# A grouped 3x3 convolution on one core: one weight tile for both pipelines, the first x rows in two pieces, the second pipeline 18 slots behind

## The chip, the cores and the metric

The kernel runs on one core of a Trainium2 chip. The metric is the device time of one execution in microseconds, and the number that counts is the median over several executions. A run's profile is that of one execution: it has a span (first to last instruction) that is a little shorter than that execution's own time.

## What is computed

`x` is 16 x 64 x 64 x 64 (image, channel, row, column), `weight` is 128 x 8 x 3 x 3, there are 8 groups, and everything is float32. Group g makes 16 output channels of 8 input channels, with a border of zeros:

```python
for g in range(groups):
    for b in range(batch):
        for co in range(16):
            for ci in range(8):
                for kh in range(3):
                    for kw in range(3):
                        output[b, g * 16 + co] += weight[g * 16 + co, ci, kh, kw] * \
                            x_pad[b, g * 8 + ci, kh:kh+h, kw:kw+w]
```

The input is 16.8 MB, the output 33.6 MB.

## The kernel before

**Tiles.** Two images have 128 channels together, so one tile holds one row of `x` (reshaped to 1024 x 4096) per partition. `xn[i]` are rows 128i to 128i+127, for i = 0 to 3: images 2i and 2i+1. `xs[i]` start at row 544 + 128i: images 8 and up, shifted by 32 partitions, so that one image's first half of channels lies in another quarter of the array than in `xn`. The missing 32 rows (512 to 543) sit in the last quarter of `xs[3]`. All are bf16 in SBUF. `ob` are eight output buffers, each of one whole image (128 channels x 4096 float32, 2 MB). The eight PSUM banks belong to two pipelines, four each.

**Loads (lines 103 to 154).** GpSimd issues 17 loads, each half of a tile (32 of 64 rows), that cast float32 to bf16 on the way; 128 partitions of them are 0.5 MB in bf16 and 1 MB read. They wait for nothing except two short waits for the masks. Two loads go another way: the first half of `xn[0]` is fetched by SP as float32 into the first half of output buffer `ob[7]` (`raw`, line 116) and is cast by ACT in two copies (line 121), and the weights are fetched on ACT's queue (line 118).

**Weight preparation (lines 158 to 187).** DVE multiplies the weights with a 0/1 mask of groups into `E`, five blocks of 32 columns for every tap (line 162). TensorE transposes 128 columns of `E` per tap, at two offsets, into PSUM (line 175): 9 transposes for `wN` and 9 for `wS`. DVE copies `wN` and ACT copies `wS` out of PSUM (line 185). The result is, per tap, a matrix of 32 input channels (four groups) by 64 output channels in each quarter.

**The main loop (lines 200 to 294).** Pipeline 0 makes images 0 to 7 from `xn` and `wN`, pipeline 1 images 8 to 15 from `xs` and `wS`. A *set* is 16 rows of an image pair: two steps j of 8 rows, two images, so four banks of 512 columns. Per tap and step, a pipeline has four matmuls of 32 x 64, one in each quarter of the array's rows; the two pipelines use the opposite halves of the columns, so eight such matmuls can be in the array at a time. The order is written out by hand in *slots*: one tap of one set, 9 slots for a set and 3 without matmuls (`PERIOD` = 12), 16 sets per pipeline. Pipeline 1 runs `LAG` = 6 slots behind, so that each evicts its banks while the other works.

After a set's last tap, `finish` (line 254) evicts four banks, ACT and DVE in turns (line 268). An eviction that begins an image pair waits for the store that last used its output buffer. After the last set of an image pair, SP issues the two stores (line 278), 16 KB per partition; for the first image pair of each pipeline (i = 0) each image is stored in two halves, 8 KB per partition. SP's queue holds the stores in program order and waits for each one's evictions. Images take the eight buffers in turn, pipeline 0's pair, then pipeline 1's.

All transfers run on the same 16 DMA engines.

Of the kernel before, what the change touches and what calls it, by code (L numbers as in the profile page):

```python
# [7 lines left out]
FP32 = mybir.dt.float32  # L8
BF16 = mybir.dt.bfloat16
ALU = mybir.AluOpType  # L10


@with_exitstack
def kernel(
    ctx: ExitStack,
    tc: tile.TileContext,
    x: bass.AP,
    weight: bass.AP,
    groups: int,
    out: bass.AP,  # L20
):
    nc = tc.nc

    B, C, H, W = x.shape
    CO, CIg, K, _ = weight.shape
    G = groups
    COg = CO // G
    HW = H * W
    T = K * K
    assert (B, C, CO, K, G, H, W) == (16, 64, 128, 3, 8, 64, 64)  # L30

    R = 8
    NCH = H // R
    HALF = HW // 2

    NOB = 8

    pool = ctx.enter_context(tc.tile_pool(name="sb", bufs=1))
    psum = ctx.enter_context(tc.tile_pool(name="psum", bufs=1, space=bass.MemoryType.PSUM))

    xn = [pool.tile([128, H, W], BF16, name=f"xn{i}") for i in range(4)]
    xs = [pool.tile([128, H, W], BF16, name=f"xs{i}") for i in range(4)]
    ob = [pool.tile([128, HW], FP32, name=f"ob{i}") for i in range(NOB)]
    w_sb = pool.tile([128, CIg * T], FP32, name="w_sb")
    mask = pool.tile([128, G], FP32, name="mask")
    ident = pool.tile([128, 128], BF16, name="ident")
    E = pool.tile([128, T, 160], BF16, name="E")
    wN = pool.tile([128, T, 128], BF16, name="wN")
    wS = pool.tile([128, T, 128], BF16, name="wS")
    banks = [psum.tile([128, 512], FP32, name=f"bank{i}") for i in range(8)]  # L50

    with tc.tile_critical():  # L52
        program(nc, x, weight, out, xn, xs, ob, w_sb, mask, ident, E, wN, wS, banks)


class Order:
# [23 lines left out]
        return self.sem, self.n  # L80


def program(nc, x, weight, out, xn, xs, ob, w_sb, mask, ident, E, wN, wS, banks):
    H = W = 64
    HW, HALF, T, G, CIg, COg, R = H * W, H * W // 2, 9, 8, 8, 16, 8
    NOB = len(ob)
# [7 lines left out]
    def sem(name):  # L94
        s = nc.alloc_semaphore(name)
        sems.append(s)
        return s
# [13 lines left out]
                landed[t.name, q, h] = (s, 16)  # L111


    raw = ob[NOB - 1][:, 0:HALF]
    s_raw = sem("raw")
    nc.sync.dma_start(raw, xr[0:128, 0:HALF]).then_inc(s_raw, 16)
    s_w = sem("w")
    nc.scalar.dma_start(w_sb, weight.rearrange("co ci kh kw -> co (ci kh kw)")).then_inc(s_w, 16)
    ACT.wait((s_raw, 16))
    for h in (0, 16):  # L120
        raw_read = ACT.done(nc.scalar.copy(  # L121
            xn[0][:, h : h + 16, :].rearrange("p h w -> p (h w)"), raw[:, h * W : (h + 16) * W],
        ))
        for q in range(4):
            for r in range(h, h + 16):
                landed[xn[0].name, q, r] = raw_read

    m1 = DVE.done(nc.vector.memset(mask, 1.0))  # L128
    m2 = DVE.done(nc.vector.memset(ident, 0.0))  # L129
    for h0, h1 in ((0, 32), (32, 64)):  # L130
        if h0 > 0:
            load(xn[0], 0, 0, 128, h0, h1)
        load(xs[0], 544, 0, 128, h0, h1)
        if h0 == 0:
            POOL.wait(m1)
            m3 = POOL.done(nc.gpsimd.affine_select(  # L136
                out=mask, in_=mask, compare_op=ALU.is_ge, fill=0.0,
                base=0, channel_multiplier=1, pattern=[[-COg, G]],
            ))
            POOL.wait(m2)  # L140
            m4 = POOL.done(nc.gpsimd.affine_select(  # L141
                out=ident, in_=ident, compare_op=ALU.not_equal, fill=1.0,
                base=0, channel_multiplier=1, pattern=[[-1, 128]],
            ))
            POOL.wait(m3)
            m5 = POOL.done(nc.gpsimd.affine_select(  # L146
                out=mask, in_=mask, compare_op=ALU.is_ge, fill=0.0,
                base=COg - 1, channel_multiplier=-1, pattern=[[COg, G]],
            ))
        load(xs[3], 512 - 96, 96, 128, h0, h1)  # L150
    for i in range(1, 4):
# [3 lines left out]

    wv = w_sb.rearrange("co (ci t) -> co t ci", t=T)
    DVE.wait((s_w, 16), m5)
    for r in range(5):  # L160
        g0 = 4 * (r % 2)
        e = DVE.done(nc.vector.tensor_mul(  # L162
            E[:, :, 32 * r : 32 * r + 32].rearrange("p t (g c) -> p t g c", c=CIg),
            wv.unsqueeze(2).to_broadcast([128, T, 4, CIg]),
            mask[:, g0 : g0 + 4].unsqueeze(1).unsqueeze(3).to_broadcast([128, T, 4, CIg]),
        ))
    PE.wait(e, m4)
    free = [None] * 8
    w_need = {}
    for k, (wt, off) in enumerate(((wN, 0), (wS, 32))):  # L170
        for g, t0 in enumerate(range(0, T, 4)):
            n = min(4, T - t0)
            b = 4 * k + g
            for t in range(n):
                ins = nc.tensor.matmul(  # L175
                    banks[b][:, 128 * t : 128 * t + 128],
                    E[:, t0 + t, off : off + 128],
                    ident,
                    start=True, stop=True,
                )  # L180
            p = PE.done(ins)
            dst = wt[:, t0 : t0 + n, :].rearrange("p t c -> p (t c)")
            eng, copy = ((DVE, nc.vector.tensor_copy), (ACT, nc.scalar.copy))[k]
            eng.wait(p)
            free[b] = eng.done(copy(dst, banks[b][:, 0 : 128 * n]))  # L185
            for t in range(n):
                w_need[wt.name, t0 + t] = free[b]

    outf = out.rearrange("b co h w -> b co (h w)")
    taps = [(1, 1)] + [(a, b) for a in range(3) for b in range(3) if (a, b) != (1, 1)]
    pe = nc.tensor
    stored = [nc.alloc_semaphore(f"st{i}") for i in range(NOB)]
    uses = [0] * NOB
# [3 lines left out]
    class Pipe:  # L200
# [5 lines left out]
        def streams(self, i):  # L206

            if self.k == 0:
                return [(q // 2, wN, xn[i], q, q % 2) for q in range(4)]
            return [  # L210
                (0, wS, xs[i], 0, 1), (1, wS, xs[i], 1, 0),
                (1, wS, xs[i], 2, 1), (0, wS, xs[i - 1], 3, 0),
            ]

        def matmuls(self, st, k, j):
# [6 lines left out]
            v0 = w0 - (kw - 1)  # L222
            nr, nw = hi - lo, w1 - w0
            left = {0: 2, 1: 2}
            for im, wt, xt, q, half in self.streams(i):
                b = self.banks[j][im]
                pos = dict(tile_position=(32 * q, 64 * half))
                w_ap = wt[32 * q : 32 * q + 32, 3 * kh + kw, 64 * half : 64 * half + 64]
                x_ap = xt[32 * q : 32 * q + 32, lo:hi, w0:w1]
                o_ap = banks[b].rearrange("p (h w) -> p h w", w=W)[  # L230
                    64 * half : 64 * half + 64, o0 : o0 + nr, v0 : v0 + nw
                ]
                if j == 0:
                    PE.wait(w_need[wt.name, 3 * kh + kw])
                    pe.ldweights(w_ap, **pos)  # L235
                PE.wait(
                    free[b] if k == 0 else None,
                    landed[xt.name, q, lo], landed[xt.name, q, hi - 1],
                )
                ins = pe.add_instruction(  # L240
                    mybir.InstMatmult(
                        name=nc.get_next_instruction_name(),
                        engine=mybir.EngineType.PE,
                        start_tensor_calc=k == 0, stop_tensor_calc=k == T - 1,
                        tile_size=(32, 64), ldweights=False, **pos,
                        ins=[pe.lower_ap(x_ap, opt=False), pe.lower_ap(w_ap, opt=False, for_matmul_weights=True)],
                        outs=[pe.lower_ap(o_ap)],
                    )
                )
                left[im] -= 1  # L250
                if k == T - 1 and left[im] == 0:
                    self.full[j, im] = PE.done(ins)

        def finish(self, st):
            i, s = st // 4, st % 4
            if s == 0:
                self.slots = [(nob[0] + im) % NOB for im in range(2)]
                self.empty = [(stored[slot], 16 * uses[slot]) if uses[slot] else raw_read for slot in self.slots]
                self.wrote = [[], []]
                nob[0] += 2  # L260
            for j in range(2):
# [7 lines left out]
                    self.wrote[im].append(free[b])  # L269
                nev[0] += 1  # L270
            nev[0] += 1
            if s == 1 and i == 0 or s == 3:
                o0, o1 = (0 if s == 1 or not (i == 0) else HALF), HALF * (s + 1) // 2
                for im in range(2):
                    slot = self.slots[im]
                    img = 2 * i + 8 * self.k + im
# [2 lines left out]
                    uses[slot] += 1  # L279

    pipes = (Pipe(0), Pipe(1))
    PERIOD, LAG, NSETS = T + 3, (T + 3) // 2, 16
    for slot in range(PERIOD * NSETS + LAG):
        live = []
        for p, lag in zip(pipes, (0, LAG)):
# [60 lines left out]
```

## Time and profile before

| What | Value |
|---|---|
| median of 9 runs | 128.67 us (128.47 to 129.14) |
| the profiled execution's own time | 128.77 us |
| its span | 127.0 us |
| TensorE busy | 86.9 us, 2322 matmuls |
| DVE, ACT, GpSimd busy | 46.1, 39.1, 9.8 us |
| HBM read and written | 16.81 MB, 33.55 MB |
| first matmul of the convolution | 11.59 us |
| first store issued | 22.52 us |
| last eviction begins | 100.28 us |

The chain that ended last, as the page gives it:

```profile
PE 45%; DMA 27%; DVE 5%; issue 1%; ACT 0%; SPq 0%; ACTq 0%; DVEq 0%
PE bank L240 43%; DMA out_dram<-ob 23%; DMA w_sb<-in_weight_dram 4%; DVE ob L268 3%; DVE E L162 2%; PE bank L175 2%; ACT ob L268 0%; ACTq L341 0%; DVEq L74 0%; SPq L278 0%; SPq L52 0%
```

The first line is by engine, the second by line of the code. The chain follows waits for semaphores; a transfer that lies behind other transfers in a queue is not resolved into them, so the time in which DMA was full has to be read from the other rows. In the rows of slices, each digit is the busy share of one fortieth of the span in tenths. GB/s counts the bytes that arrive: a casting load counts with its bf16 bytes, half of what it reads. The rows of stretches (windows) give, for each engine, busy time with its number of instructions in brackets, and then TensorE's granted clock, the mean busy share of the 16 DMA engines and GB/s. That share can pass 1 by a few per cent, since the packets of an engine overlap a little.

### The profile page before, as it was taken

The page shows a single profiled execution, that of the slowest core. Times are in us where ns is not written, and L with a number is a line of the kernel's source. Part 1 is how long each engine was busy: PE and PEld are TensorE (multiplying, and loading weights), DVE is VectorE, ACT ScalarE, POOL GpSimd, SP SyncE. Part 2 cuts the span into 40 slices and gives each one's busy share as a digit, 9 for nine tenths or more (in the row PEclk, how much of TensorE's full clock was granted, in tenths as well). Part 3 has the DMA queues.
Part 4 walks back from the last instruction along what each step waited for, and adds up shares of the span by engine and source line. Part 5 has one row for each costly group of instructions (what it writes and reads, how often), then busy time and mean ns, then how long its engine had stood idle before and what let it go on. Part 6 is the DMA issues. An engine that isn't in the chain of part 4 may idle for free.

```text
span 127.0 us, 3785 instructions
## 1 busy us (share of the span) xinstructions
PE 86.9 (68%) x2322; PEld 39.9 (31%) x1170; DVE 46.1 (36%) x74; ACT 39.1 (31%) x70; POOL 9.8 (8%) x24
## 2 busy tenths in 40 slices
PE   0009999999999989997939999999999600000000
PEld 0006425355453535452214445443354200000000
DVE  0094055445644464644224644555446500000000
ACT  4063045335433444433034633525336300000000
POOL 5995000000000000000000000000000000000000
PEclk9999999999999999999999999999999995555555
DMA  3999999999999999999999999999999999999950
GB/s 44 330 215 210 214 215 209 217 288 316 319 316 304 321 307 324 321 310 312 432 418 436 423 428 428 408 438 433 423 413 418 449 428 428 418 438 444 428 222 10
DMA packets 5375, 42.74 MB, mean 336 GB/s; under 512 B 752, under 2 KB 752, under 8 KB 2672
## 3 DMA queue, kind: packets, MB, share of 16 engines
q1 hardware_dynamic: 3024, 34.60, 65.2%
q0 software_dynamic: 2192, 7.87, 30.8%
q8 instruction: 13, 0.21, 0.6%
q10 hardware_dynamic: 144, 0.04, 0.4%
q14 instruction: 2, 0.02, 0.0%
HBM read 16.81 MB, written 33.55 MB: 396 GB/s over the span
## 4 chain that ended last, share of the span: by engine, by line
PE 45%; DMA 27%; DVE 5%; issue 1%; ACT 0%; SPq 0%; ACTq 0%; DVEq 0%
PE bank L240 43%; DMA out_dram<-ob 23%; DMA w_sb<-in_weight_dram 4%; DVE ob L268 3%; DVE E L162 2%; PE bank L175 2%; ACT ob L268 0%; ACTq L341 0%; DVEq L74 0%; SPq L278 0%; SPq L52 0%
## 5 line engine op out<-in xcount | busy, mean ns | idle before, releaser
L240 PE MATMUL bank<-xs,wS 32*64 32x504 bf16 (+3 forms) x1152 | 72.1, 373 | 3.1 <-ACT ob L268 2.1
L240 PE MATMUL bank<-xn,wN 32*64 32x504 bf16 (+3 forms) x1152 | 71.0, 376 | 0.9 <-DVE ob L268 0.9
L268 DVE COPY ob<-bank 128x512 f32<-128x512 f32 x64 | 41.5, 687 | 48.4 <-PE bank L240 42.0
L268 ACT COPY ob<-bank 128x512 f32<-128x512 f32 x64 | 34.6, 589 | 54.3 <-PE bank L240 45.9
L235 PEld LDWEIGHTS <-wS 32*64 32x64 bf16 x576 | 26.2, 104 | 23.2 <-issue 13.7
L235 PEld LDWEIGHTS <-wN 32*64 32x64 bf16 x576 | 19.2, 105 | 27.1 <-issue 22.7
L175 PE MATMUL bank<-ident,E 128*128 128x128 bf16 x18 | 2.1, 313 | 9.6 <-DVE E L162 9.6
L105 POOL DMA_DIRECT2D xs<-in_x_dram x10 | 5.7, 573 | 1.0 <-SPq L52 1.0
L162 DVE TENSOR_TENSOR E<-w_sb,mask 128x288 bf16<-128x288 f32 x5 | 2.9, 654 | 5.3 <-DMA w_sb<-in_weight_dram 5.3
L175 PEld LDWEIGHTS bank<-ident,E 128*128 128x128 bf16 x18 | 1.8, 146 | 9.6 <-DVE E L162 9.6
L105 POOL DMA_DIRECT2D xn<-in_x_dram x7 | 4.1, 581 | 0.0
L121 ACT CAST xn<-ob 128x1024 bf16<-128x1024 f32 x2 | 2.0, 1042 | 4.2 <-DMA ob<-in_x_dram 4.2
L185 ACT CAST wS<-bank 128x512 bf16<-128x512 f32 (+1 forms) x3 | 1.2, 487 | 2.3 <-PE bank L175 2.3
L185 DVE CAST wN<-bank 128x512 bf16<-128x512 f32 (+1 forms) x3 | 1.5, 550 | 0.7 <-PE bank L175 0.7
L121 ACT ACT_TABLE_LOAD x1 | 1.3, 1283 | 1.4 <-SPq L52 1.4
L128 DVE MEMSET mask<- 128x8 f32 x1 | 0.1, 65 | 1.1 <-SPq L52 1.1
L141 POOL TENSOR_SCALAR_AFFINE_SELECT ident<-ident 128x128 bf16<-128x128 bf16 x1 | 0.3, 305 | 0.0
L136 POOL TENSOR_SCALAR_AFFINE_SELECT mask<-mask 128x8 f32<-128x8 f32 x1 | 0.2, 211 | 0.1
L146 POOL TENSOR_SCALAR_AFFINE_SELECT mask<-mask 128x8 f32<-128x8 f32 x1 | 0.2, 197 | 0.0
L327 POOL MEMSET const-float32-0.0<- 128x1 f32 x1 | 0.1, 99 | 0.3 <-issue 0.3
L129 DVE MEMSET ident<- 128x64 uint32 x1 | 0.1, 112 | 0.0
L327 POOL MEMSET const-bfloat16-1.0<- 128x1 bf16 x1 | 0.1, 102 | 0.0
(2 smaller groups left out, 0.2 us busy)
## 6 DMA issues: line engine op xcount, KB each, us to landing
out_dram<-ob SPq DMA_DIRECT2D x12, 2048.0 KB, 20.2
out_dram<-ob SPq DMA_DIRECT2D x8, 1024.0 KB, 22.6
xn<-in_x_dram POOLq DMA_DIRECT2D x7, 512.0 KB, 23.0
xs<-in_x_dram POOLq DMA_DIRECT2D x6, 512.0 KB, 17.5
ob<-in_x_dram SPq DMA_DIRECT2D x1, 1024.0 KB, 5.9
xs<-in_x_dram POOLq DMA_DIRECT2D x2, 384.0 KB, 48.1
xs<-in_x_dram POOLq DMA_DIRECT2D x2, 128.0 KB, 9.3
w_sb<-in_weight_dram ACTq DMA_DIRECT2D x1, 36.0 KB, 5.6
```

The costliest lines, as they stand in the source:

```text
L105: nc.gpsimd.dma_start(t.rearrange("p h w -> p (h w)")[p0:p1, h0 * W : h1 * W], xr[row0 + p0 : row0 + p1, h0 * W : h1 * W],).then_inc(s, 16)
L121: raw_read = ACT.done(nc.scalar.copy(xn[0][:, h : h + 16, :].rearrange("p h w -> p (h w)"), raw[:, h * W : (h + 16) * W],))
L136: m3 = POOL.done(nc.gpsimd.affine_select(out=mask, in_=mask, compare_op=ALU.is_ge, fill=0.0, base=0, channel_multiplier=1, pattern=[[-COg, ...
L141: m4 = POOL.done(nc.gpsimd.affine_select(out=ident, in_=ident, compare_op=ALU.not_equal, fill=1.0, base=0, channel_multiplier=1, pattern=[ ...
L146: m5 = POOL.done(nc.gpsimd.affine_select(out=mask, in_=mask, compare_op=ALU.is_ge, fill=0.0, base=COg - 1, channel_multiplier=-1, pattern= ...
L162: e = DVE.done(nc.vector.tensor_mul(E[:, :, 32 * r : 32 * r + 32].rearrange("p t (g c) -> p t g c", c=CIg), wv.unsqueeze(2).to_broadcast([ ...
L175: ins = nc.tensor.matmul(banks[b][:, 128 * t : 128 * t + 128], E[:, t0 + t, off : off + 128], ident, start=True, stop=True,)
L185: free[b] = eng.done(copy(dst, banks[b][:, 0 : 128 * n]))
L235: pe.ldweights(w_ap, **pos)
L240: ins = pe.add_instruction(mybir.InstMatmult(name=nc.get_next_instruction_name(), engine=mybir.EngineType.PE, start_tensor_calc=k == 0, st ...
L268: free[b] = eng.done(copy(ob[slot][:, o0 : o0 + 512], banks[b]))
L327: nc = _bacc.Bacc("TRN2", target_bir_lowering=False, num_devices=1)
```

## The change

There are four edits.

- **One weight tile.** `wN` and `wS` become one tile `wt`, which both pipelines use. DVE no longer multiplies with a mask ahead of the transposes; it copies the weights, repeated 16 times, into `wb` (three copies for 4, 4 and 1 taps). TensorE transposes 9 times, and DVE multiplies with a mask of 128 x 4 as it takes the result out of PSUM (three products). The mask is made of a tile of 128 x 4 x 4 by the same two selects of GpSimd and a sum of DVE. The taps change their order to 4, 5, 6, 7, 0, 1, 2, 3, 8, and the weights are stored in that order.
- **The first x rows in two pieces.** SP fetches 8 rows and then 24 rows of `xn[0]`'s first half, after the weights' issue in the program; ACT casts them in four copies of 8 rows.
- **The first stores.** Only pipeline 0's first image pair is stored in halves; pipeline 1's first pair is stored whole like all others.
- **The lag.** `LAG` goes from 6 to 18 slots: a whole period more.

The diff, without the tiles' declarations and signatures:

```diff
@@ -111,31 +111,34 @@
                 landed[t.name, q, h] = (s, 16)
 
 
-    raw = ob[NOB - 1][:, 0:HALF]
-    s_raw = sem("raw")
-    nc.sync.dma_start(raw, xr[0:128, 0:HALF]).then_inc(s_raw, 16)
+    raw = ob[NOB - 1]
     s_w = sem("w")
     nc.scalar.dma_start(w_sb, weight.rearrange("co ci kh kw -> co (ci kh kw)")).then_inc(s_w, 16)
-    ACT.wait((s_raw, 16))
-    for h in (0, 16):
-        raw_read = ACT.done(nc.scalar.copy(
-            xn[0][:, h : h + 16, :].rearrange("p h w -> p (h w)"), raw[:, h * W : (h + 16) * W],
-        ))
-        for q in range(4):
-            for r in range(h, h + 16):
-                landed[xn[0].name, q, r] = raw_read
-
-    m1 = DVE.done(nc.vector.memset(mask, 1.0))
+    raw_read = []
+    for h0, h1 in ((0, 8), (8, 32)):
+        s_raw = sem(f"raw{h0}")
+        nc.sync.dma_start(raw[:, h0 * W : h1 * W], xr[0:128, h0 * W : h1 * W]).then_inc(s_raw, 16)
+        for h in range(h0, h1, 8):
+            ACT.wait((s_raw, 16))
+            raw_read = [ACT.done(nc.scalar.copy(
+                xn[0][:, h : h + 8, :].rearrange("p h w -> p (h w)"), raw[:, h * W : (h + 8) * W],
+            ))]
+            for q in range(4):
+                for r in range(h, h + 8):
+                    landed[xn[0].name, q, r] = raw_read[0]
+
+    m1 = DVE.done(nc.vector.memset(mask4, 1.0))
     m2 = DVE.done(nc.vector.memset(ident, 0.0))
     for h0, h1 in ((0, 32), (32, 64)):
         if h0 > 0:
             load(xn[0], 0, 0, 128, h0, h1)
         load(xs[0], 544, 0, 128, h0, h1)
         if h0 == 0:
+
             POOL.wait(m1)
             m3 = POOL.done(nc.gpsimd.affine_select(
-                out=mask, in_=mask, compare_op=ALU.is_ge, fill=0.0,
-                base=0, channel_multiplier=1, pattern=[[-COg, G]],
+                out=mask4, in_=mask4, compare_op=ALU.is_ge, fill=0.0,
+                base=0, channel_multiplier=1, pattern=[[-32, 4], [-CIg, 4]],
             ))
             POOL.wait(m2)
             m4 = POOL.done(nc.gpsimd.affine_select(
@@ -144,8 +147,8 @@
             ))
             POOL.wait(m3)
             m5 = POOL.done(nc.gpsimd.affine_select(
-                out=mask, in_=mask, compare_op=ALU.is_ge, fill=0.0,
-                base=COg - 1, channel_multiplier=-1, pattern=[[COg, G]],
+                out=mask4, in_=mask4, compare_op=ALU.is_ge, fill=0.0,
+                base=CIg - 1, channel_multiplier=-1, pattern=[[32, 4], [CIg, 4]],
             ))
         load(xs[3], 512 - 96, 96, 128, h0, h1)
     for i in range(1, 4):
@@ -155,42 +158,40 @@
 
 
 
+    taps = [(t // 3, t % 3) for t in (4, 5, 6, 7, 0, 1, 2, 3, 8)]
+    DVE.wait(m5)
+    r = DVE.done(nc.vector.tensor_reduce(
+        out=mask, in_=mask4.rearrange("p q g -> p g q"), op=ALU.add, axis=mybir.AxisListType.X,
+    ))
+    DVE.wait((s_w, 16))
     wv = w_sb.rearrange("co (ci t) -> co t ci", t=T)
-    DVE.wait((s_w, 16), m5)
-    for r in range(5):
-        g0 = 4 * (r % 2)
-        e = DVE.done(nc.vector.tensor_mul(
-            E[:, :, 32 * r : 32 * r + 32].rearrange("p t (g c) -> p t g c", c=CIg),
-            wv.unsqueeze(2).to_broadcast([128, T, 4, CIg]),
-            mask[:, g0 : g0 + 4].unsqueeze(1).unsqueeze(3).to_broadcast([128, T, 4, CIg]),
+    groups = ((0, 4, 4), (4, 0, 4), (8, 8, 1))
+    filled = [DVE.done(nc.vector.tensor_copy(
+        wb[:, k0 : k0 + n, :].rearrange("p t (g c) -> p t g c", c=CIg),
+        wv[:, t0 : t0 + n, :].unsqueeze(2).to_broadcast([128, n, 16, CIg]),
+    )) for k0, t0, n in groups]
+    PE.wait(m4)
+    free = [None] * 8
+    w_need = []
+    for b, (k0, t0, n) in enumerate(groups):
+        PE.wait(filled[b])
+        for k in range(n):
+            ins = nc.tensor.matmul(
+                banks[b][:, 128 * k : 128 * k + 128], wb[:, k0 + k, :], ident, start=True, stop=True,
+            )
+        p = PE.done(ins)
+        DVE.wait(p, r)
+        free[b] = DVE.done(nc.vector.tensor_mul(
+            wt[:, k0 : k0 + n, :].rearrange("p t (h g c) -> p (t h) g c", h=2, g=4),
+            banks[b][:, 0 : 128 * n].rearrange("p (t g c) -> p t g c", g=4, c=COg),
+            mask.unsqueeze(1).unsqueeze(3).to_broadcast([128, 2 * n, 4, COg]),
         ))
-    PE.wait(e, m4)
-    free = [None] * 8
-    w_need = {}
-    for k, (wt, off) in enumerate(((wN, 0), (wS, 32))):
-        for g, t0 in enumerate(range(0, T, 4)):
-            n = min(4, T - t0)
-            b = 4 * k + g
-            for t in range(n):
-                ins = nc.tensor.matmul(
-                    banks[b][:, 128 * t : 128 * t + 128],
-                    E[:, t0 + t, off : off + 128],
-                    ident,
-                    start=True, stop=True,
-                )
-            p = PE.done(ins)
-            dst = wt[:, t0 : t0 + n, :].rearrange("p t c -> p (t c)")
-            eng, copy = ((DVE, nc.vector.tensor_copy), (ACT, nc.scalar.copy))[k]
-            eng.wait(p)
-            free[b] = eng.done(copy(dst, banks[b][:, 0 : 128 * n]))
-            for t in range(n):
-                w_need[wt.name, t0 + t] = free[b]
+        w_need += [free[b]] * n
 
 
 
 
     outf = out.rearrange("b co h w -> b co (h w)")
-    taps = [(1, 1)] + [(a, b) for a in range(3) for b in range(3) if (a, b) != (1, 1)]
     pe = nc.tensor
     stored = [nc.alloc_semaphore(f"st{i}") for i in range(NOB)]
     uses = [0] * NOB
@@ -206,10 +207,10 @@
         def streams(self, i):
 
             if self.k == 0:
-                return [(q // 2, wN, xn[i], q, q % 2) for q in range(4)]
+                return [(q // 2, xn[i], q, q % 2) for q in range(4)]
             return [
-                (0, wS, xs[i], 0, 1), (1, wS, xs[i], 1, 0),
-                (1, wS, xs[i], 2, 1), (0, wS, xs[i - 1], 3, 0),
+                (0, xs[i], 0, 1), (1, xs[i], 1, 0),
+                (1, xs[i], 2, 1), (0, xs[i - 1], 3, 0),
             ]
 
         def matmuls(self, st, k, j):
@@ -222,16 +223,16 @@
             v0 = w0 - (kw - 1)
             nr, nw = hi - lo, w1 - w0
             left = {0: 2, 1: 2}
-            for im, wt, xt, q, half in self.streams(i):
+            for im, xt, q, half in self.streams(i):
                 b = self.banks[j][im]
                 pos = dict(tile_position=(32 * q, 64 * half))
-                w_ap = wt[32 * q : 32 * q + 32, 3 * kh + kw, 64 * half : 64 * half + 64]
+                w_ap = wt[32 * q : 32 * q + 32, k, 64 * half : 64 * half + 64]
                 x_ap = xt[32 * q : 32 * q + 32, lo:hi, w0:w1]
                 o_ap = banks[b].rearrange("p (h w) -> p h w", w=W)[
                     64 * half : 64 * half + 64, o0 : o0 + nr, v0 : v0 + nw
                 ]
                 if j == 0:
-                    PE.wait(w_need[wt.name, 3 * kh + kw])
+                    PE.wait(w_need[k])
                     pe.ldweights(w_ap, **pos)
                 PE.wait(
                     free[b] if k == 0 else None,
@@ -255,7 +256,7 @@
             i, s = st // 4, st % 4
             if s == 0:
                 self.slots = [(nob[0] + im) % NOB for im in range(2)]
-                self.empty = [(stored[slot], 16 * uses[slot]) if uses[slot] else raw_read for slot in self.slots]
+                self.empty = [(stored[slot], 16 * uses[slot]) if uses[slot] else raw_read[0] for slot in self.slots]
                 self.wrote = [[], []]
                 nob[0] += 2
             for j in range(2):
@@ -269,8 +270,8 @@
                     self.wrote[im].append(free[b])
                 nev[0] += 1
             nev[0] += 1
-            if s == 1 and i == 0 or s == 3:
-                o0, o1 = (0 if s == 1 or not (i == 0) else HALF), HALF * (s + 1) // 2
+            if s == 1 and i + self.k == 0 or s == 3:
+                o0, o1 = (0 if s == 1 or not (i + self.k == 0) else HALF), HALF * (s + 1) // 2
                 for im in range(2):
                     slot = self.slots[im]
                     img = 2 * i + 8 * self.k + im
@@ -279,7 +280,7 @@
                     uses[slot] += 1
 
     pipes = (Pipe(0), Pipe(1))
-    PERIOD, LAG, NSETS = T + 3, (T + 3) // 2, 16
+    PERIOD, LAG, NSETS = T + 3, (T + 3) // 2 + T + 3, 16
     for slot in range(PERIOD * NSETS + LAG):
         live = []
         for p, lag in zip(pipes, (0, LAG)):
```

## The prediction

> **What bounds the kernel now.** I read the page's slices first, then its queues, then stretches of the span, then the waits, and last the DMA packet records of the trace (queue, bytes, start and duration of every packet).
>
> ```profile
> PE   0009999999999989997939999999999600000000
> DMA  3999999999999999999999999999999999999950
> GB/s 44 330 215 210 214 215 209 217 288 316 319 316 304 321 307 324 321 310 312 432 418 436 423 428 428 408 438 433 423 413 418 449 428 428 418 438 444 428 222 10
> ```
>
> A slice is 3.18 us. DMA is full from the second slice to the thirty-eighth; PE stops in the thirty-second. PE is not the bound: DMA works on for some 22 us after it.
>
> ```profile
> q1 hardware_dynamic: 3024, 34.60, 65.2%
> q0 software_dynamic: 2192, 7.87, 30.8%
> q8 instruction: 13, 0.21, 0.6%
> ```
>
> q1 holds the stores (and the raw x rows), q0 the casting loads, q8 instruction fetches.
>
> ```profile
> 8.00:20.00 12.00, 10.26 (x223) 4.91 (x126) 5.57 (x10) 4.29 (x8) 3.22 (x7) 1.00 1.06 213
> 30.00:60.00 30.00, 28.78 (x800) 13.58 (x396) 14.13 (x22) 12.01 (x22) 0.00 (x0) 1.00 1.04 314
> 66.00:100.00 34.00, 33.92 (x945) 15.52 (x472) 16.85 (x26) 13.97 (x26) 0.00 (x0) 1.00 1.01 426
> 104.00:118.00 14.00, 0.00 (x0) 0.00 (x0) 0.00 (x0) 0.00 (x0) 0.00 (x0) 0.53 1.01 433
> ...
> 121.00:122.00 1.00, 0.00 (x0) 0.00 (x0) 0.00 (x0) 0.00 (x0) 0.00 (x0) 0.50 0.77 328
> 122.00:123.00 1.00, 0.00 (x0) 0.00 (x0) 0.00 (x0) 0.00 (x0) 0.00 (x0) 0.50 0.50 213
> 123.00:124.00 1.00, 0.00 (x0) 0.00 (x0) 0.00 (x0) 0.00 (x0) 0.00 (x0) 0.50 0.19 82
> 124.00:127.00 3.00, 0.00 (x0) 0.00 (x0) 0.00 (x0) 0.00 (x0) 0.00 (x0) 0.50 0.03 11
> ```
>
> The columns that matter are the last two, DMA share and GB/s. Four stages: loads alone, loads beside stores, stores with PE at work, stores alone. Then a ragged end: the 16 DMA engines carry equal bytes but do not finish together, and the last rows are one engine alone.
>
> ```profile
> SPq L74 <- DVE ob L268: 84.3, 5, 21.1
> ACT ob L268 <- DMA out_dram<-ob: 8.4, 3, 5.4
> DVE ob L268 <- DMA out_dram<-ob: 6.3, 3, 2.3
> ```
>
> SP issues stores far ahead of their transfer, and it is the evictions that wait for stores to free buffers, not DMA for data.
>
> **The sum of before, from packet records.** Per engine: 120 load packets, 64 store packets of 8 KB (the four images stored in halves), 96 of 16 KB. Eight loads take 2.455 us alone (0.307 each), eight load-and-8-KB-store pairs 4.98 us (0.622 each), eight 16 KB stores 4.86 us (0.608 each). The fastest engine has done 64 loads at 25.9 us, when the first store packet moves; the other 56 in pairs take 56 x 0.622 = 35 us, so loads end at 60.9 (seen: 60.3 to 62.3). It starts 16 KB stores at 62.8, and 96 x 0.608 = 58.4 gives 121.2 (seen 121.1). The order of the last completions is seven engines at 121.1 to 121.9, three at 122.6 to 122.8, five at 123.5 to 124.1, one at 125.44. A fetch costs its engine about 1.33 us (packet 0.94, and the next store 1.00 instead of 0.611): 13 fetches as none, one and two per engine fit these steps (3 + 5x2 = 13). The last engine is another matter. It starts its 16 KB packets at 63.4 and should end at 121.8, but 52 of its packets between 66.4 and 102.3 average 0.684 us: 52 x 0.073 = 3.8 us lost. They begin as PE resumes after its stall of 60 to 66 and cease as PE ends at 101.6. In the stage with loads no such chain exists: 8 KB stores there have a median of 0.322, and five of 862 exceed 0.335. At 62.0 to 63.4, the first pure 8 KB stores of this engine are already 0.333 to 0.347. So **one engine is slowed by running compute, only when it does nothing but store**, and it sets the end: 125.44 + 1.6 to the span's end (127.0), + 1.8 to this execution's own 128.77; the median is 128.67.
>
> **The change part by part.**
>
> *Weights.* Removed: five E products (5 x 0.654 = 2.9 us), nine of 18 transposes, three ACT evictions. Added: three copies, three products out of PSUM, a small reduce. The first matmul waits now on 6.59 (weights landed) + 2.9 + transposes and a 0.68 eviction = 11.59. Afterwards: copies of 512, 512 and 128 columns, at 0.65 for the big ones (as an E product; from 0.3 to 1.0) end near 8.0; the first product, 512 columns out of PSUM, 0.69 as the wN eviction has it (to 1.0): PE starts near 8.75, between 8 and 10. That is 2.8 us for PE and nothing for the end, as DMA hides it: cover about 20 us (below).
>
> *Raw rows in two pieces.* On SP one more issue (0.37 us) ahead of nothing that waits; the second piece starts 0.4 us later behind data already moving. Load packets begin at 5.66, as the raw packets end. 16 KB and 2 x 8 KB cost the same (0.611; 2 x 0.304), so small pieces bound at 0 to 0.15 us; I take 0. ACT has four copies instead of two, waits on the first piece, then the second; queued behind are only evictions, the first past 12 us. POOL's three selects keep their place between loads (0.2 to 0.3 us each).
>
> *Lag 18.* Twelve more slots. A pipe's period of 12 slots takes 5.04 us (ACT's evictions at 16.05 and 21.10), 0.42 a slot: PE's work ends 5.0 - 2.8 = 2 us later, less stalls. Worth 0 by itself.
>
> *Pipe 1's first images whole.* Same bytes; but while loads run, only two images' stores (32 packets per engine) are 8 KB, and after them 16 KB packets stand beside loads. Here the Trainium skill has a rule (DMA: Bandwidth & Descriptors, "Queues, rings and completion order"): an engine takes turns between queues packet by packet. The row (1:1 at equal durations) can't tell this from sharing by time. By the rule: first store at slots 0 to 20 plus eviction, near 19.3 us issued (two sets of 3.8 us, a 1 us wait for banks in between, 1.3 to evict), first packet 3.4 us later as before, 22.7; loads done (22.7 - 5.7)/0.307 = 55, left 65; 32 pairs take 19.9 us (to 42.6); 33 pairs of 0.307 + 0.608 + 0.011 = 0.93 take 30.6: loads end at 73, not 61. By time: 65 x 0.622 = 40.4, at 63. I take the packet rule.
>
> The later loads stall nobody for long: pipe 0 needs its last rows at slot 156 (74 us), pipe 1 at 174 (82 us); and DMA would not feel it. At 73 us six images' stores have moved, PE has finished ten: 4 x 8 x 0.608 = 19.5 us of stores stand ready.
>
> **The sum.** Work per engine is unchanged. What changes is how long stores are alone while PE works: before 34 us. After, at 73 us PE has done (73 - 8.75)/0.42 = 153 of 210 slots; 57 remain, 24 us. The slow engine loses 3.8 x 24/34 = 2.7 instead of 3.8: 121.8 + 2.7 = 124.4, just behind the twice-fetched engines at 124.1, which are the next bound (13 fetches for PE's program, hardly shorter). Gain 125.44 - 124.3 = 1.1: on the median, **127.5 us**.
>
> A second rule speaks against this. The same page ("Latency and other measured facts") has two DMA engines usually slower and guesses at the descriptor rings of GpSimd's loads. Then longer loading would do harm: 4.3 us late in 56 us of loads gives 5.3 in 67, so 129.7. The records are against it: slow packets start after the loads end.
>
> **The rivals.**
>
> *As above, 0.54:* 127.2 to 127.9.
>
> *Slower, 0.15: the engine is slowed beside 16 KB stores too.* Absence of slow packets in the mix may be due to short packets, whose loads let it catch up. With 33 packets at the full 0.073 it loses 2.4 more: 126.8, +1.3, so 130.0. It decides from a loss of 1.1 us, 0.033 a packet. Against it: 8 KB stores lost nothing in the mix, yet 8 to 12% at once without loads. A partial loss, 0.12, lands at 127.9 to 129.3 (faster 0.05, same 0.03, slower 0.04).
>
> *No change, 0.14: queues share by time.* Loads end at 63, PE has 81 slots left, 34 us: the loss is what it was, 128.6. Also here: a loss that depends on something else than compute.
>
> *Fetches fall otherwise, 0.05:* the bytes of PE's program shift, and an engine with two fetches is the slowed one: 124.4 + 1.3, 128.9 or more.
>
> That stores run dry (the second pipe's late start) would need PE 19 us late, and that the earlier start shows in full (125.9) would need PE to be the bound: nothing speaks for either.
>
> Some 0.2% (0.26 us) is what a measurement can tell from no change. Faster 0.59, same 0.17, slower 0.24. The range 127.1 to 129.3 leaves out most of the slower rival and a little below.
>
> **What would show it.** First matmul near 8.8; combined rates up to 73 us, 430 GB/s only from there; 13 fetches; slow store packets only after the loads, about 35; last engine near 124.3. Wrong if the loads end by 65, if packets above 0.65 appear in the mix, or if the ragged end is as long as now with another cause.

## The result and the profile after

The changed kernel takes 127.62 us (median of 10 runs, 127.45 to 128.05) beside 128.66 us for the kernel before (31 runs, one of them an outlier of 177.57): a ratio of 0.992, interval 0.9908 to 0.9932. The prediction was 127.5 us in 127.1 to 129.3. The profiled execution of the changed kernel took 128.05 us with a span of 126.3, so it lies 0.4 us above its median, where that of before lay 0.1 above. The medians differ by 1.04 us and the two profiled executions by 0.72; what follows reads the 0.72.

The slices of the changed kernel:

```profile
PE   0349989999999999999999999899997910000000
DMA  3999999999999999999999999999999999999970
GB/s 70 310 211 213 210 218 211 188 296 314 320 304 324 316 332 372 335 372 350 339 362 363 419 425 420 412 441 436 415 420 420 436 441 431 420 425 431 451 327 31
```

A slice is 3.16 us. PE starts earlier and works one slice longer; DMA is as full as it was. The row to compare is GB/s: before, 430 (stores alone) began in slice 20, at 60 us. Now there is a middle step of 340 to 370, loads beside 16 KB stores, and 420 begins only in slice 23, at 70 us. It also has a dip to 188 in slice 8, which comes up again at the end.

Stretches of the span, as before (last columns: DMA share and GB/s):

```profile
9.23:15.53 6.30, 6.30 (x68) 1.61 (x33) 0.07 (x1) 1.05 (x3) 2.65 (x6) 0.99 1.05 211
30.00:43.00 13.00, 13.00 (x384) 5.50 (x192) 6.44 (x10) 5.37 (x10) 0.00 (x0) 0.95 1.04 313
46.00:68.00 22.00, 21.74 (x615) 9.42 (x307) 11.49 (x18) 9.60 (x18) 0.00 (x0) 0.95 1.03 355
70.00:96.00 26.00, 25.65 (x680) 9.99 (x335) 12.40 (x20) 10.40 (x20) 0.00 (x0) 0.95 1.01 425
97.68:101.57 3.89, 3.89 (x68) 0.87 (x32) 0.11 (x1) 0.15 (x1) 0.00 (x0) 0.95 0.98 417
104.00:118.00 14.00, 0.00 (x0) 0.00 (x0) 0.00 (x0) 0.00 (x0) 0.00 (x0) 0.58 1.01 432
...
123.00:124.00 1.00, 0.00 (x0) 0.00 (x0) 0.00 (x0) 0.00 (x0) 0.00 (x0) 0.50 0.31 131
124.00:125.00 1.00, 0.00 (x0) 0.00 (x0) 0.00 (x0) 0.00 (x0) 0.00 (x0) 0.50 0.04 16
```

The first row is pipeline 0's first set, still alone, without its first half slot: 68 matmuls took 6.30 us. The fifth row is pipeline 1's last set, alone as well: 68 matmuls took 3.89 us. TensorE's granted clock (the third column from the right) is 0.95 in the rows from 30 to 101.57 us, where it was 1.00 in the execution of before. In the 26 us from 70 us on, 680 matmuls run; before, 945 ran in the 34 us of stores alone. At 123 to 124 us five engines' worth of DMA is at work (0.31 of 16) instead of three, and the last one stops at 124.72 instead of 125.44.

What PE and ACT waited for at the start:

```profile
ACT xn L123 <- DMA ob<-in_x_dram: 5.2, 2, 3.5
PE bank L241 <- ACT xn L123: 1.8, 1, 1.8
DVE wb L169 <- DMA w_sb<-in_weight_dram: 1.0, 1, 1.0
```

```profile
6.24 1.23 PE L241 MATMUL bank<-xn,wt 32*64 32x512 bf16 x4 [0.22 <-DVE wt L184]
9.23 6.30 PE L241 MATMUL bank<-xn,wt 32*64 32x512 bf16 x68 [1.77 <-ACT xn L123]
```

The weights, 5.6 us on their way before, landed after 3.1 us, beside x packets of 2 KB instead of 8 KB; the second piece of x took 7.0 us where the whole had taken 5.9. So the first four matmuls of the convolution, which need only rows 0 to 7, ran at 6.24 us (11.59 before). Then PE stood still for 1.77 us, until ACT had cast rows of the second piece, and went on at 9.23 us.

### The profile page after: what moved, and what is told of

Its sections match the earlier page's. It is cut to its first block, busy times and chain, and to the rows that moved or that the text cites. A ratio compares the mean times of both kernels' runs of the same rounds, so it can differ in the third digit from the quotient of the medians.

```text
span 126.3 us, 3764 instructions
## 1 busy us (share of the span) xinstructions
PE 92.7 (73%) x2313; PEld 37.1 (29%) x1161; DVE 44.4 (35%) x73; ACT 37.9 (30%) x69; POOL 10.5 (8%) x24
## 4 chain that ended last, share of the span: by engine, by line
PE 70%; DMA 6%; DVE 3%; issue 1%; ACT 0%; SPq 0%; DVEq 0%
PE bank L241 70%; DMA ob<-in_x_dram 6%; DVE ob L269 3%; ACT xn L123 0%; SPq L120 0%; SPq L342 0%; DVEq L74 0%; SPq L52 0%
## 5 line engine op out<-in xcount | busy, mean ns | idle before, releaser
L241 PE MATMUL bank<-xn,wt 32*64 32x504 bf16 (+3 forms) x1152 | 75.8, 393 | 3.0 <-ACT xn L123 1.8
L241 PE MATMUL bank<-xs,wt 32*64 32x504 bf16 (+3 forms) x1152 | 72.3, 382 | 1.0 <-ACT ob L269 0.5
L236 PEld LDWEIGHTS <-wt 32*64 32x64 bf16 x1152 | 36.3, 107 | 58.8 <-issue 46.5
L105 POOL DMA_DIRECT2D xs<-in_x_dram x10 | 6.3, 633 | 1.0 <-SPq L52 1.0
L179 PE MATMUL bank<-ident,wb 128*128 128x128 bf16 x9 | 1.2, 303 | 4.9 <-DVE wb L169 4.9
L123 ACT CAST xn<-ob 128x512 bf16<-128x512 f32 x4 | 2.3, 615 | 5.2 <-DMA ob<-in_x_dram 5.2
L179 PEld LDWEIGHTS bank<-ident,wb 128*128 128x128 bf16 x9 | 0.8, 130 | 5.0 <-issue 4.8
L169 DVE CAST wb<-w_sb 128x512 bf16<-128x512 f32 (+1 forms) x3 | 1.3, 508 | 1.0 <-DMA w_sb<-in_weight_dram 1.0
L184 DVE TENSOR_TENSOR wt<-bank,mask 128x512 bf16<-128x512 f32 (+1 forms) x3 | 1.5, 551 | 0.1
```

What stands on the lines that cost most here:

```text
L105: nc.gpsimd.dma_start(t.rearrange("p h w -> p (h w)")[p0:p1, h0 * W : h1 * W], xr[row0 + p0 : row0 + p1, h0 * W : h1 * W],).then_inc(s, 16)
L123: raw_read = [ACT.done(nc.scalar.copy(xn[0][:, h : h + 8, :].rearrange("p h w -> p (h w)"), raw[:, h * W : (h + 8) * W],))]
L169: filled = [DVE.done(nc.vector.tensor_copy(wb[:, k0 : k0 + n, :].rearrange("p t (g c) -> p t g c", c=CIg), wv[:, t0 : t0 + n, :].unsqueeze ...
L179: ins = nc.tensor.matmul(banks[b][:, 128 * k : 128 * k + 128], wb[:, k0 + k, :], ident, start=True, stop=True,)
L184: free[b] = DVE.done(nc.vector.tensor_mul(wt[:, k0 : k0 + n, :].rearrange("p t (h g c) -> p (t h) g c", h=2, g=4), banks[b][:, 0 : 128 * n ...
L241: ins = pe.add_instruction(mybir.InstMatmult(name=nc.get_next_instruction_name(), engine=mybir.EngineType.PE, start_tensor_calc=k == 0, st ...
```

## The experiments

Theory 1 is that of the prediction: one DMA engine loses time for what PE does after the loads have ended, that engine ends last, and 16 KB stores beside the loads push the end of the loads back. Theory 2 holds that PE's earlier start is the gain, theory 3 that the lag is.

The measure in all of them comes from the packet records: for the slowed engine (the one that ends last, save in e1, e7, e10 and e12), the sum of (duration - 0.611 us) over its slow 16 KB store packets (0.63 to 0.76 us; those next to a fetch lie above that, and in e8, where they are more uneven, I followed the engine's chain of packets instead), the *loss*. Beside it stand the matmuls and weight loads of PE in the stretch from the first to the last of these packets (in e3, e7 and e12 from the end of the loads), the time at which half of the engines have finished their loads, and the last two engines' ends. All of this is from one profiled execution of each kernel. The ratios come from the medians: each is taken against runs of the kernel before made beside it, whose medians lay between 128.50 and 128.69, so compare kernels by their ratios.

| Kernel | loads end | matmuls + weight loads | loss, us | last two engines | median, us | ratio to before (interval) |
|---|---|---|---|---|---|---|
| before | 60.8 | 940 + 460 | 3.79 | 124.07, 125.44 | 128.67 | |
| changed | 70.2 | 772 + 376 | 3.13 | 124.39, 124.72 | 127.62 | 0.992 (0.9908 to 0.9932) |
| e3 whole stores only | 67.5 | 908 + 444 | 3.52 | 124.21, 124.88 | 128.09 | 0.9967 (0.9953 to 0.998) |
| e4 lag only | 62.0 | 980 + 483 | 3.95 | 124.29, 125.51 | 128.85 | 1.0018 (1.0009 to 1.0027) |
| e5 preparation and x only | 64.6 | 916 + 452 | 3.72 | 124.60, 125.54 | 128.69 | 1.0015 (1.0006 to 1.0023) |
| e1 changed, lag 6 | 73.6 | 624 + 307 | 2.64 | 124.53, 124.60 | 127.84 | 0.9946 (0.993 to 0.9963) |
| e2 changed, halves | 62.0 | 976 + 479 | 3.94 | 124.66, 125.96 | 128.53 | 1.000 (0.9989 to 1.0012) |
| e11 whole stores and lag | 67.1 | 866 + 420 | 3.49 | 124.20, 124.72 | 128.06 | 0.9967 (0.9953 to 0.998) |
| e6 all stores whole | 65.1 | 883 + 436 | 3.52 | 124.11, 124.28 | 127.89 | 0.9957 (0.9941 to 0.9974) |
| e10 e6, quarter loads | 76.1 | 608 + 292 | 2.50 | 124.11, 124.37 | 127.72 | 0.9929 (0.9911 to 0.9946) |
| e12 changed, quarter loads | 93.7 | 332 + 160 | (below) | 124.89, 125.02 | 128.06 | 0.9966 (0.9955 to 0.9977) |
| e7 one tap of nine | 69.5 | 60 + 28 | 0.22 | 122.46, 123.18 | 126.34 | 0.982 (0.9806 to 0.9834) |
| e8 small taps | 65.8 | 932 + 460 | 3.63 | 124.36, 125.46 | 128.68 | 1.0003 (0.9993 to 1.0013) |
| e9 few weight loads | 61.3 | 932 + 48 | 2.79 | 123.75, 124.13 | 127.49 | 0.991 (0.9893 to 0.9926) |

**The three parts of the change, apart.** e3:

```diff
-            if s == 1 and i == 0 or s == 3:
+            if s == 1 and i + self.k == 0 or s == 3:
```

(and the same condition for `o0`).

> The kernel before with one edit: the second pipeline's first image pair is stored whole. Theory 1 (one DMA engine loses about 3.9 ns per matmul that runs after the loads have ended, and sets the end; 16 KB packets beside loads push the end of the loads back): loads end near 68 us instead of 62, 750 to 900 matmuls remain instead of 985, the slow engine loses 2.9 to 3.5 us instead of 3.8, and the time is 127.7 to 128.4 us. Theory 2 (the earlier start of the convolution is the gain): 128.7, no change. Theory 3 (the lag is the gain): 128.7, no change.

128.09: the one condition brings 0.33% by itself, as theory 1 says; 2 and 3 fall as the only cause. The later end of the loads shows in its slices, where the step of 335 to 370 GB/s has come in before the 430 of stores alone:

```profile
GB/s 47 346 210 211 216 216 207 216 254 311 315 308 317 324 337 342 370 343 363 335 370 408 430 430 420 420 430 425 430 425 414 440 430 420 440 420 446 430 269 26
```

e4:

```diff
-    PERIOD, LAG, NSETS = T + 3, (T + 3) // 2, 16
+    PERIOD, LAG, NSETS = T + 3, (T + 3) // 2 + T + 3, 16
```

> The kernel before with one edit: lag 18 instead of 6, both first pairs in halves. Theory 1: all store packets beside loads are 8 KB, so loads end near 62 us as before, and some 1000 matmuls remain: 128.6 to 129.0, no gain. Theory 3 (the lag is the gain): about 127.6. Theory 2: 128.7 or more.

128.85, slower by 0.18%: the lag alone leaves more of PE's work to the time after the loads (980 matmuls).

e5 is the changed kernel with both of these lines as they were before.

> The new weight preparation and the x rows in two pieces, with the lag of 6 and both first pairs in halves as before. Theory 1: first matmul near 9.2 us, loads end at 61 to 63, the loss is about what it was: 128.4 to 128.8. Theory 2 (the earlier start is the gain): about 127.6 or less.

128.69, slower by 0.15%. The earlier start alone is no gain.

e1 has only the lag of the two put back:

> The changed kernel with the lag put back to 6. Theory 1: the whole stores do it, so loads end at 68 to 70 us and about 700 to 850 matmuls remain: 127.5 to 128.1, near the changed kernel (127.6). Theory 3 (the lag is the gain): 128.7. Theory 2: 127.6.

127.84, with the fewest matmuls left of these four kernels. In its profile the slowed engine (loss 2.64) no longer stands apart from those with two fetches (124.53), so a smaller loss could not show. But e1 is not even level with the changed kernel, whose loss is larger by 0.49: the ratios are 0.9946 and 0.992, and their intervals only just meet. Whether the lag brings something of its own beside the new preparation and the whole stores, the runs don't settle.

e2 has only the halves put back in the changed kernel:

> The changed kernel with the second pipeline's first pair in halves again (new preparation and lag 18 stay). Theory 1: loads end at 62 to 64 us, 900 to 1000 matmuls remain, loss 3.7 to 4.0: 128.5 to 129.0. Rival (the lag or the preparation is the gain, alone or together): 127.6.

128.53, and a ratio of 1.000: without the whole stores the gain is gone, and so is the step in the slices:

```profile
GB/s 63 327 211 213 211 215 215 182 283 313 328 302 317 317 317 308 322 310 322 389 439 424 426 421 432 424 432 416 426 432 421 421 437 426 442 421 437 426 221 10
```

e11 is e3 and e4 together, so the change without the preparation and the pieces of x:

> The kernel before with the lag of 18 and the second pipeline's first pair stored whole, with the old weight preparation and the x rows in one piece: the change without its first two edits. Theory 1: loads end at 68 to 71 us, 780 to 900 matmuls remain, loss 3.1 to 3.5: 127.6 to 128.0, near the changed kernel (127.6). If the new preparation carries a part of the gain of its own: 128.2 or more.

128.06, between the two forecasts. The ratio decides: 0.9967 (0.9953 to 0.998) lies clear of the changed kernel's 0.992 (0.9908 to 0.9932), so the first two edits have a share, though alone, with stores in halves (e5), they gain nothing. In e11 the first store packet moved 0.9 us later (26.2 us against 25.3) and the loads ended 3 us earlier, so 866 matmuls were left and not 772: 3.49 - 3.13 = 0.36 us more loss, where the medians differ by 0.44. That would fit theory 1, with the early start at work only through what is then not left for the time of stores alone. But the two profiled executions ended at the same 124.72 us, so the traces don't show it. The weight tile and the x rows in two pieces were not tried apart.

**What in the compute slows the engine.** e7 leaves eight of nine taps out of the slots (only the main line of the edit is shown; the first tap now also ends a set):

```diff
-            if 0 <= st < NSETS and k < T:
+            if 0 <= st < NSETS and k == 0:
```

> The kernel before with one tap of nine: eight ninths of the matmuls and weight loads of the main loop are left out, so its output is not the convolution; loads, evictions and stores are all there. If PE's instructions slow the engine: fewer than 150 matmuls remain after the loads, loss under 0.6 us, and with some 2 instruction fetches instead of 13 no engine ends late: 125.0 to 125.8. If the evictions slow it (28 on DVE and on ACT after the loads): loss about 3.8 and 128.3 to 128.7.

e8 keeps all instructions and takes most of the data away from those of eight taps:

```diff
+                if k > 0:
+                    hi, nr, w1, nw = lo + 1, 1, w0 + 8, 8
```

> The kernel before with eight of the nine taps cut to 8 columns of one row: as many matmuls and weight loads as before, but almost nothing streams through in them, and the output is not the convolution. If the number of PE's instructions slows the engine, some 1000 or more remain after the loads: loss 3.8 or more, 128.5 to 129.5. If it is the data that PE streams or PE's busy time: loss under 1 us, the engines with two fetches end last, 127.0 to 127.5. If evictions: 128.5.

e9 keeps all matmuls and takes eight of nine weight loads away:

```diff
-                if j == 0:
+                if j == 0 and k == 0:
                     PE.wait(w_need[wt.name, 3 * kh + kw])
```

> The kernel before with the weights loaded for the first tap of a set alone (128 weight loads instead of 1152; the other eight taps multiply with the first tap's weights, so the output is not the convolution). All matmuls, evictions, loads and stores are there. PE's program is about 1000 instructions shorter: 9 or 10 fetches instead of 13. If every instruction of PE counts (940 matmuls and 460 weight loads after the loads, 3.8 us): 940 and 50 remain, loss 2.6 to 2.8, end of the last engine near 124.3, 127.3 to 127.7 us. If only matmuls count: loss 3.6 to 3.9, 128.3 to 128.7.

The same stretch of stores alone, in e7, e8 and e9 in this order (PE, PEld, DVE, ACT with their instructions):

```profile
66.00:100.00 34.00, 11.52 (x84) 2.89 (x39) 14.31 (x24) 11.67 (x24) 0.00 (x0) 0.60 1.01 423
```

```profile
66.00:100.00 34.00, 22.09 (x951) 12.12 (x472) 18.05 (x28) 14.98 (x29) 0.00 (x0) 1.00 1.01 424
```

```profile
66.00:100.00 34.00, 33.85 (x925) 3.17 (x48) 16.73 (x26) 13.96 (x26) 0.00 (x0) 0.95 1.01 428
```

e7 has nearly all evictions of this stretch (24 of 26) and a loss of 0.22: the evictions are not the cause. e8 has PE busy for 22 us instead of 34 and the full loss, 3.63, and its time is that of before: the data that PE streams is not the cause. e9 has PE as busy as before and a loss of 2.79: weight loads count like matmuls. Loss by PE's instructions is 3.79/1400 = 2.7 ns before, 2.6 in e8, 2.8 in e9, 2.5 in e7, and 2.6 to 2.9 in e1 to e6, e10 and e11. So it is **the number of PE's instructions, not its work**, as far as recorded executions show: every timed run on record has a span and a granted clock, so the recording was on in all of them, and whether it is itself the traffic that costs so much an instruction is untested. PE's program also has to be fetched, 13 times before; e9 and e7:

```profile
q8 instruction: 9, 0.15, 0.4%
```

```profile
q8 instruction: 1, 0.02, 0.0%
```

With one fetch, 15 of 16 engines of e7 end within 121.6 to 122.5, and the steps of 1.3 us between engines are gone; with nine fetches (e9), some engine must get two if they go around eight engines, as the steps of before suggest. e7's 126.34 is above the 125.0 to 125.8 expected: even its least delayed engines end at 121.6, not 121.1. e9's 1.2 us go with fewer instructions (1.0 us less loss, and 9 fetches for 13), but its output lacks the other taps' weights.

**Can more be had?** e6 makes the first pipeline's first pair whole too:

```diff
-            if s == 1 and i + self.k == 0 or s == 3:
-                o0, o1 = (0 if s == 1 or not (i + self.k == 0) else HALF), HALF * (s + 1) // 2
+            if s == 3:
+                o0, o1 = 0, HW
```

> The changed kernel with the first pipeline's first pair stored whole too, so that every store packet is 16 KB. Theory 1: the first store packet moves near 34 us instead of 25, some 94 of 120 loads are done by then, 26 pairs of 0.925 us put the end of the loads at 58 to 59 us (not 70), about 1070 matmuls remain, the slow engine loses 4.2 to 4.4 us: 128.9 to 129.4, slower than the kernel before. A rival (larger store packets are themselves what is gained): 127.4 or less, at most the changed kernel's time.

127.89: faster than before where I expected slower. Half of the miss is in the table: the first store packet moved at 32.4 us and the loads ended at 65, so 883 matmuls were left, not 1070, and 2.7 ns for each of 1319 instructions give 3.5 us, as seen. The rest is not the loss: this kernel's least delayed engines ended at 120.9, against 121.1 before and 121.6 in the changed kernel. Fewer loads beside stores (35 pairs instead of 56, at 0.011 each) would make 0.2 of it; the remainder is open. "Larger packets themselves" can't be ruled out as a small part.

e10 is e6 with loads of 16 rows for the last image pair of each pipeline, e12 the changed kernel with the same:

```diff
-        for h0, h1 in ((0, 32), (32, 64)):
+        n = 32 if i < 3 else 16
+        for h0, h1 in [(h, h + n) for h in range(0, 64, n)]:
```

> The changed kernel with all stores whole (as in e6) and the loads of the last image pair in quarters of a tile instead of halves: 56 load packets of half the size per engine for 28, each of which again stands beside a 16 KB store. Theory 1: loads end near 82 us instead of 65, about 400 matmuls remain instead of 883, the slow engine loses 1.6 us and ends near 122.5, and the engines with two instruction fetches (124.0 in e6) end last: 127.2 to 127.6, faster than the changed kernel's 127.6 or the same, and faster than e6 (127.9). If the convolution is held up by late rows: 128 or more. If the loss doesn't depend on when the loads end: 127.9 as e6.

> The changed kernel, its stores as they are, with the loads of the last image pair in quarters of a tile. Theory 1: loads end at 83 to 88 us, 300 to 400 matmuls remain, the slow engine loses some 1.4 us and is no longer the last; the engines with two fetches (124.2 to 124.4 in the changed kernel) end last: 127.2 to 127.6. If the last rows come too late for the convolution and the stores run short: 128 or more.

e10 measured 127.72, 0.12 above the range: loads ended at 76 us instead of 82, 608 matmuls were left, and the loss was 2.50 where 2.7 ns an instruction give 2.43. It is level with the changed kernel and not better. e12 measured 128.06. After its loads the slow packets (1.5 us in sum) are spread over several engines, so no loss stands in the table; the loads now came too late:

```profile
PE bank L242 <- DMA xn<-in_x_dram: 7.3, 2, 4.0
...
GB/s 80 337 207 215 212 211 164 281 322 317 311 311 312 350 355 363 391 376 392 375 364 378 372 377 404 374 392 371 387 391 436 420 347 435 440 435 425 420 420 41
```

PE waited 7.3 us for rows of `xn`, stores ran short (347 in slice 33), and even the least delayed engine ended at 123.5, some 2 us later. This is the rival of late rows. No full kernel that I tried beats the changed one.

## Why the prediction was right, step by step

**Right: DMA is the bound and the last engine sets the end.** It ended 0.72 us earlier in the profile, and the loss fell by 0.66.

**Partly luck: the number.** I forecast a gain of 1.1 us and the medians differ by 1.04, but the traces show 0.72; 0.3 us of the gain is in no trace. The profiled execution of the changed kernel had a clock of 0.95 from 14 to 106 us. At 1.00, PE would have done 5% more in the 56 us up to the end of the loads, some 120 instructions, worth 0.3 us of loss: an estimate from the rows above, which no second trace confirms.

**Right: queues take turns by packet.** In the records, eight pairs of a load and a 16 KB store took 7.1 to 7.4 us, so about 0.92 a pair against 0.93 worked out. Sharing by time would have ended the loads at 63; they ended at 70.

**Right: no slow packets beside loads.** In the changed kernel, 16 KB stores between 48 and 65 us have a median of 0.624, and apart from those next to a fetch none exceeds 0.63. The rival "slowed beside 16 KB stores too" is out. The Trainium skill's guess at GpSimd's descriptor rings (DMA: Bandwidth & Descriptors, "Latency and other measured facts"), which spoke against the change, does not fit either: the longer load phase went with a shorter time.

**Right in sum, wrong in two terms.** The first is PE's pace. I took 0.42 us for every slot. Most slots took little more, lone ones too: 0.46 in the last set (3.89 us for 8.5 slots), at a clock of 0.95. But at the start of its work PE was slow: until 14 us a matmul took 0.60 to 0.63 us, and 0.37 to 0.39 from then on, so those 8.5 slots took 6.30 us in the first set. So the first store packet came at 25.3 us instead of 22.7, 61 loads and not 55 were done by then, and loads ended at 70, not 73. PE ended at 101.6 and not near 97, for the same slow start and for the clock of 0.95 (e10, which has the same slots, ended at 100.4 at a clock of 1.00). PE's work left after the loads was 31 us, not 24.

The second term is the price of that work. I had it per microsecond, which would make 3.8 x 31/34 = 3.5 us of 31 us. It is per instruction, and the last 15 slots with matmuls (6 before) are lone ones, which carry half as many: 1148 instructions at 2.7 ns give the 3.13 us that were lost. My 2.7 us came out near it because the two errors were of opposite sign.

**Wrong: PE's start.** I let PE wait for weights until 8.75 us. They were there at 4.1 us and the first matmuls ran at 6.24; what PE then waited for was the second piece of x, to which I had given no cost. In e1, e5 and e12, which start in the same way, ACT could cast it 2 us earlier and PE did not stop, so this varies from one execution to another. What it did to the end was not measured by itself.

**Right: the next bound.** Engines with two fetches ended at 124.16 to 124.39, 0.3 us ahead of the last, and 13 fetches stayed 13. That would explain why e1 and e10, with less loss, gain nothing more; e6, whose slowed engine ended at 124.28, stands at the same bound.

## What to carry to other kernels

When all DMA engines are full from start to end, equal bytes do not mean equal ends: look at the ragged last microseconds, follow the last engine's packets back, and ask what else that engine had to serve. Where two queues share the engines packet by packet, packet size sets how fast each is served, and one condition on a store can move the end of the loads by 7 to 9 us (here e3 beside before, the changed kernel beside e2, e1 beside e5). And an earlier start of compute may be worth nothing by itself under a full DMA, as in e5.

## What the hardware showed that I had not expected

- One DMA engine of 16 loses 2.5 to 2.9 ns for every PE instruction while it does nothing but store (16 KB packets of 0.66 to 0.68 us instead of 0.611), and nothing that shows while loads stand between its stores. Which traffic of PE's it serves, the records don't show. It may be the recording of PE's instructions: an execution without any recording was not tried, and if that is it, the gain would be smaller without it.
- At the start of its work on the convolution PE is slow: the first 8 matmuls before, the first 52 in the changed kernel and 16 to 60 in the other full kernels take about 0.60 to 0.63 us instead of 0.36 to 0.39. In each of these traces the first record of the granted clock stands within 0.8 us behind the last slow one (12.8 us before, 14.3 in the changed kernel). So a lower clock up to there is likely, but what was granted ahead of the first record isn't in the traces.
- After that, a pipeline alone takes about as long for a slot as two together (0.43 us before, 0.46 in the changed kernel): the second pipeline's matmuls take hardly any time of their own.
- Around the first store packet, load packets take 0.4 to 0.7 us instead of 0.324 for some 2 to 6 us: 10 packets with 1.1 us too much before, 44 with 8.1 in the changed kernel, 74 with 12.2 in e1 (sums over 16 engines, so 0.1 to 0.8 us each). It is the dip to 188 GB/s. The time of the first store alone doesn't set it: in e2 that is 25.9 us, as before, and packets over 0.4 us there have 11 us too much. I have no cause for it.
